# A bias table made by one product of rounded numbers over 97 stacked rows instead of an fp32 product over 33

## The chip, the cores and the metric

The kernel runs on one core of one Trainium2 chip. The metric is device time in microseconds (us): the median of several executions, beside the time of the kernel before on the same chip. One further execution of each kernel is recorded by the hardware profiler, and the rows below come from that one.

## What is computed

One layer of a decoder block on 512 tokens of width 1024, all in fp32: block-sparse attention beside a pooling mixer, then a gated feed-forward part with a short convolution. The change touches only the bias that attention adds to its logits. It depends on head and distance alone:

```
bias_t = rel_bias.T
bias_own = bias_t[:, t5_bucket(dist_own)]
logit_own = jnp.einsum('bhqd,bhkd->bhqk', qc, k_own) * scale + bias_own
logit_own = jnp.where(dist_own >= 0, logit_own, -jnp.inf)
```

`rel_bias` holds 32 buckets for each of 8 heads.

## The kernel before

Matrix products on TensorE (PE) work on numbers that are split in two: a rounded part (type `fp32r`, "hi") and what the rounding left ("lo"). A product is then three passes, hi times hi, hi times lo, lo times hi (`mm3`, lines 127 to 130), and ScalarE (ACT) makes the hi parts while VectorE (DVE) makes the lo parts, ahead of their use. All instructions of PE, DVE and ACT stand in the order in which the program is written; each engine works through its own row of them. POOL (GpSimd) takes small powers and some DMA issues, SP issues most loads.

The program goes through these stages: the adaLN sums and the projections `p` and `q` (to about 61 us), the projection `k` with the pooling arithmetic and the bias table inside it (61 to 86 us), the projection `v` and the first logits, the eight heads interleaved with the gate projections, the branch products, the output projection, and the feed-forward part from about 315 us on.

The bias table is computed for 640 distances and 8 heads. `table` in memory has 33 rows: a one-hot matrix with the entry -1 at each distance's bucket (row 32 marks the distances that are masked), and beside it the 32 bucket values and 1e30. Lines 332 to 337 put three slots of SBUF aside, `hot_0` (512 columns), `hot_1` (128) and `rel` (8), and SP loads them from `table`. `bias_table()` (lines 210 to 215) makes two products, called `fp` in the trace, of `rel` (33x8, fp32) and `hot` (33x512 and 33x128, fp32). Each goes to a bank of PSUM, ACT copies it to the tile `f`, and POOL issues its DMA to the scratch tensor `fd`, from which each head later reads its bias (`trev`, line 434).

Where it stands: `fill(kgen, us)` hands PE a few steps of the projection `k`. Between those calls the program issues the split of the pooling weights (`pwh`, `pwl`, lines 554 and 555), two pooling groups, the normalised queries `n_q` (`head_norm`, line 385), and then `bias_table()` (line 564), so that the two `fp` products stand in the middle of the k projection's third weight unit. The two banks that `fp` writes are those from which the first and the second `n_q` instruction read: in the built program the first `fp` product waits for the first `n_q`, the second for the second.

Of the kernel before, what the change touches and what calls it, by code (L numbers as in the profile page):

```python
# [7 lines left out]
F32 = mybir.dt.float32  # L8
F32R = mybir.dt.float32r
AF = mybir.ActivationFunctionType  # L10
# [8 lines left out]
H = 8  # L19
# [4 lines left out]
NB = 32  # L24
EPS = 1e-6
WINDOWS = (2, 4, 8, 16)
BIG = 1e30
NF = 640
NG = 16
AW = D + 2  # L30
FIRST = 5.2
# [20 lines left out]
def block_kernel(tc, x, cvec, ada, wtok, wch, pool_w, wbr, wout, wup, wdn, pack, table, out):  # L52
    nc = tc.nc
# [3 lines left out]
    with ctx:  # L57
# [11 lines left out]
        def slot(name, dt=F32, w=512):  # L69
            return sp.tile([P, w], dt, tag="s", name=name)  # L70

        def bank(name):
            return psp.tile([P, 512], F32, tag="b", name=name)
# [11 lines left out]
        plan += [(wtok[8 + i], f"v{i}") for i in range(4)]  # L85
        plan += [(wch[i], f"gate{i}") for i in range(NG)]
        for j in range(8):
            if 8 + j >= NG:
                plan.append((wch[8 + j], f"gate{8 + j}"))
# [117 lines left out]

        fd = dpool.tile([H, NF], F32, name="fd")

        def bias_table():  # L210
            for i, (c0, n) in enumerate(((0, 512), (512, NF - 512))):
                fp = bank(f"fp_{i}")
                nc.tensor.matmul(fp[:H, :n], rb_[: NB + 1, :H], hot[i][: NB + 1, :n], start=True, stop=True)
                nc.scalar.activation(fsb[i][:H, :n], fp[:H, :n], AF.Copy)
                nc.gpsimd.dma_start(fd[:, c0 : c0 + n], fsb[i][:H, :n])

# [92 lines left out]
        for k in range(KT):  # L309
            i = k // 2  # L310
            if k % 2 == 0:
                pw, qw = ready.pop(f"p{i}"), ready.pop(f"q{i}")
            c0 = (k % 2) * 512
# [15 lines left out]
            mm3s([(qps[t], hh[k][:, tslice(t)], hl[k][:, tslice(t)], qw[0][:, ws], qw[1][:, ws])  # L329
                  for t in range(TT)], k == 0, k == KT - 1, late=1)  # L330

        hot = [slot("hot_0"), slot("hot_1")]
        rb_ = slot("rel")
        fsb = [slot("f_0"), slot("f_1")]
        nc.sync.dma_start(rb_[: NB + 1, :H], table[:, NF:])
        for i, (c0, n) in enumerate(((0, 512), (512, NF - 512))):
            nc.sync.dma_start(hot[i][: NB + 1, :n], table[:, c0 : c0 + n])

        def tok_proj(i, ps, name):
            for kk in range(4):  # L340
# [9 lines left out]
        def gate_proj(i, store, name):  # L350
            w = unit(name)
            ps = bank(f"{name}_ps")
            for k in range(KT):
                mm3(ps, w[0][:, tslice(k)], w[1][:, tslice(k)], hh[k], hl[k], k == 0, k == KT - 1)
                yield 0.65
            g = slot(name)
            nc.scalar.activation(g, ps, AF.Copy)
            store[i] = g

        def fill(gen, us):  # L360
            while us > 0:
                c = next(gen, None)
                if c is None:
                    return
                us -= c
# [185 lines left out]
        nc.sync.dma_start(pk[:, C_EARLY:], pack[:, C_EARLY:])  # L551
        nc.sync.dma_start(pwr, pool_w)
        fill(kgen, 1)
        nc.scalar.activation(pwh, pwr, AF.Copy)
        nc.vector.tensor_sub(pwl, pwr, pwh.bitcast(F32))
        fill(kgen, 3)
# [5 lines left out]
        pooling(2)  # L562
        fill(kgen, 1)
        bias_table()
        fill(kgen, 1)
        for g in range(2):
# [36 lines left out]
        def gate_stream():  # L603
            for i in range(NG):
                yield from gate_proj(i, gates, f"gate{i}")

        gg = gate_stream()
        fill(gg, FIRST)
        share = (NG * 5.2 - FIRST) / H
        for h in range(H):  # L610
# [345 lines left out]
def _bucket(d):  # L956
    if d < 16:
        return d
    return min(31, 16 + int(math.log(d / 16) / math.log(8.0) * 16))


def _layout(a):
    f = {k: np.asarray(v) for k, v in a.items()}
    one = lambda k: f[k][0]
    c = np.ascontiguousarray
    arr = {}
    arr["x"] = c(f["x"][0])
    arr["cvec"] = c(f["c"])
    unit = np.zeros((6, D, 1), np.float32)
    unit[[1, 4]] = 1.0  # L970
    arr["ada"] = c(np.concatenate(
        [one("ada_w").T, one("ada_b")[:, None], unit.reshape(6 * D, 1)], axis=1)).reshape(48, P, AW)
    w = one("w_in")
    tok = w[:, :2048].reshape(4, 2, P, 4, 512)
    arr["wtok"] = c(tok.transpose(3, 0, 2, 1, 4)).reshape(16, P, 1024)
    ch = lambda m, kt: m.reshape(kt, P, -1, P).transpose(2, 1, 0, 3)
    arr["wch"] = c(ch(w[:, 2048:], KT)).reshape(16, P, 1024)
    arr["pool_w"] = c(one("pool_w").transpose(1, 0, 2)).reshape(P, 512)
    wa, wb = ch(one("w_branch_attn"), 4), ch(one("w_branch_pool"), 4)
    arr["wbr"] = c(np.concatenate([wa, wb], axis=2)).reshape(8, P, 1024)  # L980
    tokm = lambda m: c(m.reshape(m.shape[0] // 256, 2, P, 2, 512).transpose(0, 3, 2, 1, 4)).reshape(-1, P, 1024)
    arr["wout"] = tokm(one("w_out"))
    up = ch(one("w_up"), KT).reshape(2, NP, P, 1024)
    arr["wup"] = c(up.transpose(1, 0, 2, 3)).reshape(2 * NP, P, 1024)
    dn = one("w_down").reshape(NP // 2, 2, P, 2, 512)
    blocks = np.stack([dn[:, 0, :, 0], dn[:, 0, :, 1], dn[:, 1, :, 1], dn[:, 1, :, 0]])
    blocks = np.concatenate([blocks, np.zeros((4, 2 * NU - NP // 2, P, 512), np.float32)], axis=1)
    arr["wdn"] = c(blocks.reshape(4, NU, 2, P, 512).transpose(0, 1, 3, 2, 4)).reshape(4, NU, P, 1024)
    cols = lambda v: v.reshape(-1, P).T
    qk = lambda k: np.concatenate([one(k), one(k)])[:, None]  # L990
    inv = np.zeros((P, 64), np.float32)
    for g, wd in enumerate(WINDOWS):
        inv[:, 16 * g : 16 * g + 16] = 1.0 / np.minimum(np.arange(16) + 1, wd)
    cw = one("conv_w").reshape(3, 2 * NP, P).transpose(2, 1, 0).reshape(P, -1)
    arr["pack"] = c(np.concatenate(
        [cols(one("norm1_g")), cols(one("norm2_g")), qk("q_norm_g"), qk("k_norm_g"),
         cols(one("pool_scale")), inv, np.eye(P, dtype=np.float32), cw, cols(one("conv_b"))], axis=1))
    hot = np.zeros((NB + 1, NF), np.float32)
    for i in range(NF):
        hot[NB if i < 127 else _bucket(i - 127), i] = -1.0  # L1000
    rb = np.concatenate([f["rel_bias"], np.full((1, H), -BIG, np.float32)], axis=0)
    arr["table"] = c(np.concatenate([hot, rb], axis=1))
    return arr


# [20 lines left out]
```

## Time and profile before

| what | value |
|---|---|
| median of 3 runs | 674.45 us (673.62 to 675.25) |
| the profiled execution | 673.66 us, of which the span is 671.7 us |
| PE busy | 659.7 us, 98% of the span |
| DVE busy | 517.0 us, 77% |
| ACT busy | 332.0 us, 49% |
| POOL busy | 93.3 us, 14% |
| granted TensorE clock | 1.000 in the whole span |

The span is the time from the first to the last instruction of the profiled execution; its own time is 1.96 us more. PE rows are matrix products, PEld rows the loads of their stationary operand, which run beside them. In a row of time the first number is the start in us from the span's start, the second the duration; "x4" means that four like instructions are merged. What stands in brackets is the idle time of that engine before the row, and what ended it.

### The profile page before, as it was taken

What the parts mean: (1) busy time and instruction counts of PE and PEld (TensorE: products, weight loads), DVE (VectorE), ACT (ScalarE), POOL (GpSimd) and SP (SyncE); (2) the same over time, 40 slices, a digit from 0 to 9 for tenths busy, and PEclk for the clock granted to TensorE, in tenths of its full rate; (3) what the DMA queues carried; (4) which work ended last, traced back from release to release, by engine and by line L of the source; (5) the groups of instructions that cost most, each with busy time, mean ns of one, the idle gap of its engine ahead of it and who ended that gap; (6) DMA issues with size and microseconds to landing.
All of it is one profiled execution on the core that took longest, in us unless ns stands there. A gap on an engine that the chain in (4) does not pass through costs nothing.

```text
span 671.7 us, 8748 instructions
## 1 busy us (share of the span) xinstructions
PE 659.7 (98%) x3090; PEld 548.5 (82%) x3090; DVE 517.0 (77%) x854; ACT 332.0 (49%) x532; POOL 93.3 (14%) x125
## 2 busy tenths in 40 slices
PE   6999999999999999999999999999999999999997
PEld 3778788888888787888998888888888888888885
DVE  5795876887877688867578878888777878878774
ACT  6555256766564655504653443424343344767431
POOL 3002140000000054703011111120110001001000
PEclk9999999999999999999999999999999999999999
DMA  8785231354543286693367675966845446867651
GB/s 309 290 344 186 94 128 64 111 170 169 173 147 110 94 182 229 226 354 125 107 212 251 226 253 191 305 226 218 298 142 186 163 151 128 292 224 270 244 182 58
DMA packets 41889, 131.48 MB, mean 196 GB/s; under 512 B 5379, under 2 KB 5548, under 8 KB 41846
## 3 DMA queue, kind: packets, MB, share of 16 engines
q1 hardware_dynamic: 35270, 109.82, 48.8%
q0 software_dynamic: 6576, 21.12, 9.4%
q8 instruction: 24, 0.39, 0.2%
q14 instruction: 19, 0.16, 0.1%
HBM read 115.16 MB, written 15.76 MB: 195 GB/s over the span
## 4 chain that ended last, share of the span: by engine, by line
PE 90%; DVE 3%; DMA 3%; ACT 2%; issue 2%; SPq 0%; DVEq 0%; ACTq 0%
PE u L128 12%; PE u L130 12%; PE u L129 12%; PE gate_ps L129 4%; PE gate_ps L128 4%; PE gate_ps L130 4%; PE X L893 3%; PE X L891 3%; PE X L892 3%; PE o L128 2%; PE o L129 2%; PE o L130 2%; DMA raw_ada<-in_ada 2%; DVE raw_ada L191 2%; PE O L495 2%
## 5 line engine op out<-in xcount | busy, mean ns | idle before, releaser
L128 PE MATMUL u<-h2h,hi_up 128*128 128x512 f32 (+1 forms) x384 | 142.7, 372 | 0.0
L129 PE MATMUL u<-h2l,hi_up 128*128 128x512 f32 (+1 forms) x384 | 142.6, 371 | 0.0
L130 PE MATMUL u<-h2h,lo_up 128*128 128x512 f32 (+1 forms) x384 | 142.6, 371 | 0.0
L130 PEld LDWEIGHTS u<-h2h,lo_up 128*128 128x128 f32 x384 | 72.3, 188 | 12.6
L129 PEld LDWEIGHTS u<-h2l,hi_up 128*128 128x128 f32 x384 | 72.3, 188 | 12.5
L128 PEld LDWEIGHTS u<-h2h,hi_up 128*128 128x128 f32 x384 | 72.3, 188 | 12.4
L191 DVE CUSTOM_DVE_ANT_0 raw_ada<-raw_ada,cbc 128x1026 f32<-128x1026 f32 x48 | 58.8, 1250 | 6.1 <-DMA raw_ada<-in_ada 3.2
L761 ACT ACTIVATE uv<-u,pk 128x512 f32<-128x512 f32 x22 | 17.2, 780 | 85.8 <-PE u L130 85.8
L119 DVE TENSOR_TENSOR lo_up<-raw_up,hi_up 128x1024 fp32r<-128x1024 f32 x44 | 52.0, 1218 | 4.8 <-ACT hi_up L109 4.8
L130 PE MATMUL gate_ps<-h_h,lo_gate 128*128 128x512 f32 x128 | 49.9, 390 | 0.0
L129 PE MATMUL gate_ps<-h_l,hi_gate 128*128 128x512 f32 x128 | 49.9, 390 | 0.0
L128 PE MATMUL gate_ps<-h_h,hi_gate 128*128 128x512 f32 x128 | 49.9, 390 | 0.0
L109 ACT ACTIVATE hi_up<-raw_up 128x1024 fp32r<-128x1024 f32 x44 | 44.2, 1048 | 4.3 <-PE u L129 4.3
L814 POOL DMA_DIRECT2D tsum_t<-b x44 | 23.8, 540 | 145.1 <-DVE b L809 139.0
L762 DVE SCALAR_TENSOR_TENSOR uv<-u,pk,uv 128x511 f32<-128x511 f32 x22 | 16.5, 749 | 34.2 <-ACT uv L761 34.2
L119 DVE TENSOR_TENSOR lo_t<-raw_t,hi_t 128x1024 fp32r<-128x1024 f32 (+1 forms) x24 | 26.6, 1131 | 9.1 <-ACT hi_t L109 9.1
L761 ACT ACTIVATE ug<-u,pk 128x512 f32<-128x512 f32 x22 | 17.0, 775 | 32.2 <-PE u L130 32.2
L109 ACT ACTIVATE hi_t<-raw_t 128x1024 fp32r<-128x1024 f32 (+1 forms) x24 | 23.7, 987 | 17.9 <-PE Y L893 8.8
L204 POOL TENSOR_TENSOR wo_l<-raw_wo,wo_h 128x512 fp32r<-128x512 f32 x16 | 25.6, 1621 | 20.2 <-ACT wo_h L203 20.2
L130 PEld LDWEIGHTS gate_ps<-h_h,lo_gate 128*128 128x128 f32 x128 | 24.0, 188 | 5.1
L128 PEld LDWEIGHTS gate_ps<-h_h,hi_gate 128*128 128x128 f32 x128 | 24.0, 188 | 4.6
L129 PEld LDWEIGHTS gate_ps<-h_l,hi_gate 128*128 128x128 f32 x128 | 24.0, 188 | 4.5
(253 smaller groups left out, 1505.4 us busy)
## 6 DMA issues: line engine op xcount, KB each, us to landing
raw_ada<-in_ada SPq DMA_DIRECT2D x48, 513.0 KB, 5.0
raw_up<-in_wup SPq DMA_DIRECT2D x44, 512.0 KB, 4.9
b<-in_wdn SPq DMA_DIRECT2D x44, 256.0 KB, 5.9
tsum_t<-b POOLq DMA_DIRECT2D x44, 256.0 KB, 3.0
raw_t<-tsum_t SPq DMA_DIRECT2D x20, 512.0 KB, 4.5
raw_gate<-in_wch SPq DMA_DIRECT2D x16, 512.0 KB, 5.0
raw_b<-in_wdn SPq DMA_DIRECT2D x15, 512.0 KB, 3.8
raw_br<-in_wbr SPq DMA_DIRECT2D x8, 512.0 KB, 4.4
```

The source lines that it names most:

```text
L109: nc.scalar.activation(hi, raw, AF.Copy)
L119: nc.vector.tensor_sub(lo, raw, hi.bitcast(F32))
L128: nc.tensor.matmul(ps, sh, mh, start=start, stop=False)
L129: nc.tensor.matmul(ps, sh, ml, start=False, stop=False)
L130: nc.tensor.matmul(ps, sl, mh, start=False, stop=stop)
L191: nc.vector.tensor_tensor_reduce(out=raw, in0=raw, in1=cbc, op0=ALU.mult, op1=ALU.add, scale=1.0, scalar=0.0, accum_out=acol[:, i : i + 1])
L204: (eng or nc.vector).tensor_sub(lo[:, :w], src, hi[:, :w].bitcast(F32))
L761: nc.scalar.activation(t, ps, AF.Identity, scale=cw(2), bias=col(C_CB + i))
L814: nc.gpsimd.dma_start(tsum[n, i][:, u * 512 : u * 512 + 512], b[nm])
L891: nc.tensor.matmul(ps, sh, mh, start=start, stop=False, skip_group_check=True)
L892: nc.tensor.matmul(ps, sh, ml, start=False, stop=False, skip_group_check=True)
L893: nc.tensor.matmul(ps, sl, mh, start=False, stop=stop, skip_group_check=True)
```

## The change

The table in memory becomes 97 rows: the 33 rows, 31 rows of zeros, and the 33 rows again. SP loads all 97 of them, the one-hot part to new slots `hotr`. ACT rounds the 97x8 bucket values to `rels`; DVE overwrites rows 64 to 96 of `rels` with what the rounding left. DVE also copies the one-hot parts to `fp32r` (its entries are 0 and -1). The products then take 97 rows in which rounded part and low part meet the same one-hot matrix, so that one product of rounded numbers adds both.

```
+NT = 64 + NB + 1
...
-                nc.tensor.matmul(fp[:H, :n], rb_[: NB + 1, :H], hot[i][: NB + 1, :n], start=True, stop=True)
+                nc.tensor.matmul(fp[:H, :n], rbs[:NT, :H], hot[i][:NT, :n], start=True, stop=True)
...
-        hot = [slot("hot_0"), slot("hot_1")]
+        hot = [slot("hot_0", F32R), slot("hot_1", F32R)]
+        hotr = [slot("hotr_0"), slot("hotr_1")]
+        rbs = slot("rels", F32R)
         rb_ = slot("rel")
         fsb = [slot("f_0"), slot("f_1")]
-        nc.sync.dma_start(rb_[: NB + 1, :H], table[:, NF:])
+        nc.sync.dma_start(rb_[:NT, :H], table[:, NF:])
         for i, (c0, n) in enumerate(((0, 512), (512, NF - 512))):
-            nc.sync.dma_start(hot[i][: NB + 1, :n], table[:, c0 : c0 + n])
+            nc.sync.dma_start(hotr[i][:NT, :n], table[:, c0 : c0 + n])
...
         fill(kgen, 1)
+        nc.scalar.activation(rbs[:NT, :H], rb_[:NT, :H], AF.Copy)
+        nc.vector.tensor_sub(rbs[64:NT, :H], rb_[64:NT, :H], rbs[64:NT, :H].bitcast(F32))
+        for i, n in enumerate((512, NF - 512)):
+            nc.vector.tensor_copy(hot[i][:NT, :n], hotr[i][:NT, :n])
         nc.scalar.activation(pwh, pwr, AF.Copy)
         nc.vector.tensor_sub(pwl, pwr, pwh.bitcast(F32))
...
-    arr["table"] = c(np.concatenate([hot, rb], axis=1))
+    tab = np.concatenate([hot, rb], axis=1)
+    arr["table"] = c(np.concatenate([tab, np.zeros((64 - NB - 1, NF + H), np.float32), tab], axis=0))
```

On DVE the three added instructions stand between the low part of the third k unit (`lo_k`) and that of the pooling weights (`pwl`). Before:

```order
L375 TENSOR_SCALAR hs_q_639<-hs_q_639 128x8
L119 TENSOR_TENSOR lo_k_655<-raw_k_651,hi_k_653 128x1024
L555 TENSOR_TENSOR pwl<-pwr,pwh 128x512
L520 TENSOR_TENSOR pd_1_680<-pt_608 128x511
L521 COPY pd_1_680<-pt_608 128x1
```

and in the changed kernel:

```order
L379 TENSOR_SCALAR hs_q_642<-hs_q_642 128x8
L120 TENSOR_TENSOR lo_k_658<-raw_k_654,hi_k_656 128x1024
L559 TENSOR_TENSOR rels<-rel,rels 33x8
L561 CAST hot_588<-hotr_590 97x512
L561 CAST hot_589<-hotr_591 97x128
L563 TENSOR_TENSOR pwl<-pwr,pwh 128x512
L524 TENSOR_TENSOR pd_1_687<-pt_611 128x511
L525 COPY pd_1_687<-pt_611 128x1
```

All that follows on DVE, `n_q` among it, stands three instructions later; nothing else has moved there. On ACT one instruction (`rels`, 97x8) stands between the rounded parts of that k unit and of the pooling weights.

On PE the two products keep their place in the k projection; in brackets are the semaphores that each waits for (DMAHW: a load). Before:

```order
L130 MATMUL k_646<-hi_k_653,h_l 128x512
L213 MATMUL fp_793<-hot_588,rel 8x512 [waits DMAHW7_49,DMAHW6_49,DVE_49]
L213 MATMUL fp_797<-hot_589,rel 8x128 [waits DMAHW0_49,DVE_49]
L128 MATMUL k_647<-hi_k_653,h_h 128x512
```

and in the changed kernel:

```order
L131 MATMUL k_649<-hi_k_656,h_l 128x512
L214 MATMUL fp_800<-hot_588,rels 8x512 [waits DVE_49,Activation_49]
L214 MATMUL fp_804<-hot_589,rels 8x128 [waits DVE_49]
L129 MATMUL k_650<-hi_k_656,h_h 128x512
```

Neither product waits for a load any more; both wait for DVE as before, the first also for ACT's `rels`. SP's and POOL's queues hold the same instructions in the same order, three of SP's loads with 97 rows in place of 33.

## Rows read from the trace of the kernel before

**Rows 1.** The page: span, PE's busy time, and the chain that ended last by engine.
```profile
span 671.7 us, 8748 instructions
...
PE 659.7 (98%) x3090; PEld 548.5 (82%) x3090; DVE 517.0 (77%) x854; ACT 332.0 (49%) x532; POOL 93.3 (14%) x125
...
PE 90%; DVE 3%; DMA 3%; ACT 2%; issue 2%; SPq 0%; DVEq 0%; ACTq 0%
```

**Rows 2.** Waits of PE in the whole span, longest and shortest: us, times, longest.
```profile
PE cb L230 <- ACT crow L150: 3.2, 1, 3.2
...
PE B L130 <- DVE lo_br L119: 0.2, 1, 0.2
```

**Rows 3.** PE in order of time around the bias products: the first k product, then 77 to 80.6 us.
```profile
61.68 0.39 PE L128 MATMUL k<-hi_k,h_h 128*128 128x512 f32 x1
...
77.10 0.39 PE L130 MATMUL k<-hi_k,h_l 128*128 128x512 f32 x1
77.42 1.24 PE L213 MATMUL fp<-hot,rel 33*8 33x512 f32 x4
78.59 0.50 PE L128 MATMUL k<-hi_k,h_h 128*128 128x512 f32 x1
78.92 0.40 PE L129 MATMUL k<-lo_k,h_h 128*128 128x512 f32 x1
...
80.30 0.39 PE L129 MATMUL pw<-pool_l,pwh 128*128 128x512 f32 x1
```

**Rows 4.** PE in order of time, the narrow products of rounded numbers of one head.
```profile
124.52 0.22 PE L495 MATMUL O<-PT_h,v 128*128 128x128 f32 x1
124.58 0.27 PE L495 MATMUL O<-PT_l,v 128*128 128x128 f32 x1
124.69 0.33 PE L495 MATMUL O<-PT_h,v 128*128 128x256 f32 x1
```

**Rows 5.** Waits from 60 to 100 us: the loads of `fp` for the normalised queries.
```profile
PEld fp L213 <- DVE n_q L385: 0.7, 2, 0.4
```

**Rows 6.** DVE instructions grouped by shape: total us, mean ns, idle before.
```profile
L385 DVE TENSOR_TENSOR n_q<-q,hr_q 128x512 f32<-128x512 f32 x4 | 2.5, 679 | 0.0
L468 DVE TENSOR_SCALAR L<-L,ri 128x128 f32<-128x128 f32 x8 | 2.3, 287 | 0.3
...
L555 DVE TENSOR_TENSOR pwl<-pwr,pwh 128x512 fp32r<-128x512 f32 x1 | 0.7, 689 | 0.0
L107 DVE CAST hi_p<-raw_p 128x1024 fp32r<-128x1024 f32 x1 | 0.7, 687 | 0.0
...
L526 DVE TENSOR_TENSOR fx<-pd,pk 128x2 f32<-128x2 f32 x1 | 0.2, 160 | 0.0
```

**Rows 7.** DVE in order of time, 63 to 98 us.
```profile
63.34 0.17 DVE L375 TENSOR_SCALAR hs_q<-hs_q 128x8 f32<-128x8 f32 x1
...
66.18 0.69 DVE L555 TENSOR_TENSOR pwl<-pwr,pwh 128x512 fp32r<-128x512 f32 x1
...
75.18 2.47 DVE L385 TENSOR_TENSOR n_q<-q,hr_q 128x512 f32<-128x512 f32 x4
...
97.08 0.74 DVE L415 SCALAR_TENSOR_TENSOR Q<-T_True,qgn,Q 64x512 fp32r<-64x512 f32 x1 [2.04 <-ACT Q L414]
```

**Rows 8.** ACT in order of time, 64 to 69 us.
```profile
64.08 0.65 ACT L554 ACTIVATE pwh<-pwr 128x512 fp32r<-128x512 f32 x1
68.57 0.63 ACT L203 ACTIVATE pool_h<-pool 128x512 fp32r<-128x512 f32 x1 [3.84 <-DVE pool L527]
```

**Rows 9.** SP's queue in order of time: the loads of the one-hot matrix.
```profile
51.16 0.72 SPq L337 DMA_DIRECT2D hot<-in_table  x2
```

**Rows 10.** DMA issues: KB each, median us to landing; the pooling weights.
```profile
pwr<-in_pool_w SPq DMA_DIRECT2D x1, 256.0 KB, 6.6
```

**Rows 11.** DVE in order of time, where the branch stage begins.
```profile
228.54 0.69 DVE L204 TENSOR_TENSOR PT_l<-PT,PT_h 128x512 fp32r<-128x512 f32 x1 [2.32 <-ACT PT_h L203]
```

**Rows 12.** POOL in order of time: the powers for the queries.
```profile
62.87 6.88 POOL L377 TENSOR_TENSOR hr_q<-hs_q,mhalf 128x8 f32<-128x8 f32 x4 [48.72 <-DVE hs_q L375]
```

## The prediction

> **What bounds the kernel now.** I read the page first. PE is busy for 659.7 of the 671.7 us and the chain that ended last is PE for 90% [rows 1]: the end moves by what PE's own stream of instructions gains or loses, and hardly by anything else. Then the waits of PE: seven groups in the whole span, the longest 3.2 us at the start, the shortest 0.2 us [rows 2], and none of them at the bias products. So the question is how long the two `fp` products hold PE, and whether what the change puts on DVE makes PE wait where it does not wait now. For the first I read PE in order of time around them, for the second DVE's own stream up to the `n_q` instructions that `fp` stands behind.
>
> **What the products cost now.** In the k projection 69 products of 512 columns start from 61.68 to 77.10, one every 0.227 us, so behind the last of them the next place is 77.33. The eighth product behind `fp` starts at 80.30 [rows 3]; without `fp` it would start at 77.33 + 7 x 0.227 = 78.92. The two fp32 products therefore cost PE 80.30 - 78.92 = 1.38 us. They are four passages in the trace ("x4", 1.24 us).
>
> **What they cost after.** Their operands are then of the type of the k projection, so 512 columns should take the 0.227 us of a k product. For 128 columns the nearest rows are the narrow products of attention: starts 0.06 and 0.11 us apart [rows 4], so rounded numbers do not become slow at 128 columns. What I can't read is what the change of shape costs on either side. Lower bound: 0.227 + 0.06 = 0.29 us. Upper bound: the product behind `fp` now starts 0.33 instead of 0.227 us ahead of its successor [rows 3], and I allow that 0.10 us on both sides and 0.11 for the narrow one: 0.227 + 0.11 + 0.20 = 0.54 us. I take 0.40, the middle. **Term: 1.38 - 0.40 = 0.98 us less on PE**, between 0.84 and 1.09.
>
> The Trainium skill has another way to that term: "FP8 and Floating Point Precision", section "TensorE Precision Notes", says that a true fp32 product takes four passes through the array. With one pass in place of four, 3 x 640 columns at the 0.443 ns a column of a k product go away, an estimate of 0.85 us; the row has 1.38 us where four such passes would be 1.13, so the rule misses what the switch costs, and I stay with the rows.
>
> **What is added on DVE.** Three instructions ahead of `pwl`, at 66.2 us. The subtraction on 33x8: 0.16 us, as the small ones [rows 6]. The copies to `fp32r` are not there in this shape; the nearest is the copy of 1024 columns, 687 ns, and a one-input instruction of 128 columns, 287 ns [rows 6]. The line through these two gives 0.45 ns a column: 0.46 us for 512 and 0.29 for 128, together with the subtraction 0.91 us at most, since DVE starts the next instruction some 0.08 us ahead of the end of the last (four `n_q` of 0.68 us take 2.47, so they start 0.60 apart [rows 6, 7]). I take 0.7 us. Lower bound: the 640 columns alone and the subtraction, 0.29 + 0.16 = 0.45 us; upper bound, if the copies went at the pace of a two-input instruction (689 ns for 512 columns [rows 6]), 0.16 + 0.69 + 0.29 = 1.14 us. DVE has no wait for others here that would swallow this: its pooling arithmetic goes to and fro with ACT, which waits for it for 3.84 us [rows 8]. So all of it arrives at `n_q`.
>
> **What hides it.** The first `n_q` runs from 75.18 to 75.86, the second ends at 76.46 [rows 7]. The first `fp` product can't start before 77.33, the second, 512 columns later, not before 77.56. Slack: 1.47 and 1.10 us. The wait that the trace puts on `n_q` is that of the loads of `fp`'s stationary operand, 0.7 us in two [rows 5]; PE itself does not wait, and 76.46 lies far ahead. With 0.7 us on DVE, `n_q` ends at 77.16: hidden, with 0.4 us to spare. At the upper bound it would be 77.60, 0.04 us late. If the cover were gone, each further us on DVE would be one on PE. Behind `fp`, DVE's lateness ends at 97.08, where it waits 2.04 us for ACT, which waits for PE's transposes [rows 7].
>
> The other additions cost nothing. ACT rounds 97x8 ahead of `pwh` at 64.08, some 0.2 us, and then waits 3.84 us for DVE anyway [rows 8]. The loads carry 97 rows for 33, 165 KB more; they are issued at 51.2 us [rows 9] and wanted at 66.2, and 256 KB issued in this stretch landed in 6.6 us [rows 10].
>
> **Does the gain reach the end?** PE's waits after 80 us are 0.2 us each [rows 2]. The one stage in which DVE and ACT lead, the branch products from 228 to 264 us, starts with DVE idle for 2.32 us, released by ACT behind PE's transposes [rows 11]; it starts earlier by what PE gains.
>
> **The sum.** 673.66 us of the profiled execution - 0.98 = 672.7. The median of the runs is 674.45, 0.8 above that execution; I predict for the median: 674.45 - 0.98 = **673.4 us**, -0.15%. About 0.2%, 1.35 us, is what a measurement of this kernel can tell from no change; its three runs lie 1.6 us apart.
>
> **Rivals.**
>
> *The copies stand behind POOL* (slower). At 66.3 us, when DVE comes to the copies, POOL works on the powers `hr_q`, from 62.87 until 69.75 [rows 12]. If a one-input copy could not run until POOL is done, DVE would be late by 69.75 - 66.3 + 0.7 = 4.1 us, the second `n_q` would end at 80.6 instead of 76.46, and PE, ready at 77.56, would stand for 3.0 us: 674.45 - 0.98 + 3.0 = 676.5 us. It decides from 1.10 us of lateness on, and the kernel is slower from 1.10 + 0.98 = 2.1 us on. Against it: three one-input `hs_q` instructions (the first at 63.34) run in those same 6.88 us and take 0.17 us each [rows 7, 12]; they have 8 columns only. The rule behind it is in the Trainium skill, "SBUF — State Buffer", section "Who interferes with whom": a copy or cast on VectorE may take the port pair that it shares with GpSimd, whoever issues first has it for the whole instruction, and the other is blocked. No row here shows a long copy beside a power. Chance 0.08.
>
> *The gain is lost again in a later stage*: DVE, 77% busy, leads somewhere and doesn't start earlier. For it: the 0.2 us for `lo_br` at the end of the branch stage [rows 2]. Against it: the 2.32 us of rows 11. The time would be 674.4 us. Chance 0.08.
>
> *The change doesn't do what it says*: with 8 output rows and 97 stacked rows the product still goes in four passages and costs 1.38 us. Against it, all other products of rounded numbers, at 0.227 us. 674.4 us. Chance 0.04.
>
> **How the numbers follow.** The forecast holds 0.80. Within it the scatter decides what a measurement calls it: 0.37 us more gain than the forecast would be over 0.2%, so 0.18 of the 0.80 goes to faster, 0.60 to same and 0.02 to slower. The two rivals at 674.4 us give 0.02 to faster, 0.09 to same and 0.01 to slower; POOL's gives 0.07 to slower and 0.01 to same. Faster 0.20, same 0.70, slower 0.10. The range: the forecast with its bounds is 673.3 to 673.6, the scatter of a median adds 0.8 either way, and the two rivals at 674.4 with 0.8 reach 675.2: 672.3 to 675.2. POOL's rival and the tails are left out.
>
> **What the profile would show.** Right: the `fp` row as two passages, and 0.3 to 0.5 us between the last k product before it and the place of the next; copies of some 0.4 and 0.25 us on DVE at 66 us; `n_q` 0.5 to 0.9 us later; no wait of PE at `fp`; everything from 80 us on about 1 us earlier. Wrong: `fp` in four passages, a copy of more than 1 us or an idle DVE beside POOL's powers, a wait of PE for `n_q`, or a branch stage that starts earlier but ends at the old time.

## The result and the profile after

| | before | after |
|---|---|---|
| median of the runs compared | 674.45 us (673.26 to 675.25) | 677.95 us (677.85 to 680.31) |
| profiled execution, span | 673.66, 671.7 us | 677.85, 675.6 us |

Ratio 1.0066, 95% interval 1.0055 to 1.0077: **slower by 0.66%** (the medians lie 3.50 us apart), outside the range, against a forecast of a small gain. The page of the changed kernel: PE is as busy as before within 2 us, but PE's part of the chain that ended last fell from 90% [rows 1] to 79%, and the parts of DMA, DVE and ACT grew.

```profile
span 675.6 us, 8746 instructions
PE 661.6 (98%) x3088; PEld 550.0 (81%) x3088; DVE 517.7 (77%) x857; ACT 331.8 (49%) x533; POOL 92.9 (14%) x125
PE 79%; DMA 8%; DVE 6%; ACT 3%; issue 2%; SPq 1%; POOL 0%; DVEq 0%; ACTq 0%
```

PE in order of time around the bias products, which answers to [rows 3] (start us, duration us, engine, line, instruction; in brackets the idle time ahead of it and its releaser):

```profile
start us, us, engine line op out<-in xcount [idle before <-releaser]
77.28 0.39 PE L131 MATMUL k<-hi_k,h_l 128*128 128x512 f32 x1
80.11 0.79 PE L214 MATMUL fp<-hot,rels 97*8 97x512 f32 x2 [2.44 <-DVE n_q L389]
80.69 0.74 PE L129 MATMUL k<-hi_k,h_h 128*128 128x512 f32 x1
81.22 0.63 PE L130 MATMUL k<-lo_k,h_h 128*128 128x512 f32 x1
...
82.93 0.55 PE L131 MATMUL k<-hi_k,h_l 128*128 128x512 f32 x1
83.31 0.40 PE L129 MATMUL pw<-pool_h,pwh 128*128 128x512 f32 x1
83.55 0.39 PE L130 MATMUL pw<-pool_l,pwh 128*128 128x512 f32 x1
```

Most of the loss can be read here, with the same counting as in the prediction. The next place behind the last k product is 77.28 + 0.23 = 77.51, and without `fp` the eighth product would start at 79.10. It starts at 83.55, so `fp` costs 4.45 us where it cost 1.38: 2.60 us of standing, 0.58 us for the products (two passages now), and 1.27 us in the products behind them, which start 0.43 us apart until 82.93 and not 0.23. The granted clock over the same stretch says why these are so slow:

```profile
core 0: us, PE busy (x) PEld busy (x) DVE busy (x) ACT busy (x) POOL busy (x), PEclk, DMA share, GB/s
78.00:80.00 2.00, 0.00 (x0) 0.00 (x0) 1.87 (x3) 1.05 (x2) 0.00 (x0) 0.96 0.00 0
80.00:83.00 3.00, 2.89 (x8) 1.99 (x9) 3.00 (x5) 0.00 (x0) 0.00 (x0) 0.50 0.51 175
83.00:86.00 3.00, 3.00 (x14) 2.51 (x13) 2.86 (x9) 0.00 (x0) 0.00 (x0) 0.96 0.49 175
```

PE stood, then ran at 0.50, the 1.2 GHz level, and was back near 1.0 behind 83 us. 4.45 - 1.38 = 3.07 us; with 0.18 us by which this run was late already ahead of `fp`, PE is 3.25 us behind at the eighth product and keeps that, within 0.1 us, until 576 us. There it loses 0.7 us more, in the down projection; none of the profiles read below shows a loss there, and its cause stays open. The half clock isn't part of every execution: one of the five has a granted clock of 1.000 and takes 677.95 us, no less than the others.

Why was `n_q` late? ACT and DVE ahead of it, where the split of the pooling weights `pwh`, `pwl` stood at 64.08 and 66.18 [rows 7, 8]:

```profile
start us, us, engine line op out<-in xcount [idle before <-releaser]
66.49 0.16 DVE L559 TENSOR_TENSOR rels<-rel,rels 33x8 fp32r<-33x8 f32 x1
66.67 0.56 DVE L561 CAST hot<-hotr 97x512 fp32r<-97x512 f32 x2
...
69.62 0.63 ACT L562 ACTIVATE pwh<-pwr 128x512 fp32r<-128x512 f32 x1 [5.13 <-DMA pwr<-in_pool_w]
70.28 0.69 DVE L563 TENSOR_TENSOR pwl<-pwr,pwh 128x512 fp32r<-128x512 f32 x1 [3.05 <-ACT pwh L562]
...
79.28 2.48 DVE L389 TENSOR_TENSOR n_q<-q,hr_q 128x512 f32<-128x512 f32 x4
```

The added DVE work took what was forecast (0.7 us), and lies in time that DVE would have stood anyway: behind it DVE waits 3.05 us more, because the load of `pwr` had not landed. SP's queue in order of time (columns as above), which issued the one-hot loads in 0.72 us before [rows 9]. What followed them before:

```profile
51.98 3.42 SPq L77 DMA_DIRECT2D raw_v<-in_wtok  x3
55.45 0.42 SPq L552 DMA_DIRECT2D pwr<-in_pool_w  x1
```

and in the changed kernel:

```profile
51.00 0.28 SPq L339 DMA_DIRECT2D rel<-in_table  x1
51.34 2.87 SPq L341 DMA_DIRECT2D hotr<-in_table  x2
54.30 7.03 SPq L78 DMA_DIRECT2D raw_v<-in_wtok  x3
61.38 0.52 SPq L556 DMA_DIRECT2D pwr<-in_pool_w  x1
```

`pwr` is issued 5.9 us later; the first of the three `raw_v` issues alone takes 5.73 us, where each took 0.33 to 0.35 before. From 55 to 60 us the DMA engines are all but idle. Stretches of the changed kernel (columns as above; the last two are the DMA share and GB/s):

```profile
54.00:56.00 2.00, 2.00 (x11) 1.65 (x10) 1.89 (x3) 0.38 (x1) 0.00 (x0) 1.00 0.15 54
56.00:58.00 2.00, 2.00 (x10) 1.67 (x9) 0.00 (x0) 0.00 (x0) 0.00 (x0) 1.00 0.07 26
58.00:60.00 2.00, 2.00 (x10) 1.67 (x9) 0.00 (x0) 1.33 (x3) 0.00 (x0) 1.00 0.07 26
60.00:62.00 2.00, 2.00 (x10) 1.65 (x10) 0.00 (x0) 1.35 (x4) 0.00 (x0) 1.00 0.61 229
```

and of the kernel before:

```profile
54.00:56.00 2.00, 2.00 (x10) 1.67 (x9) 1.11 (x2) 0.00 (x0) 0.00 (x0) 1.00 0.98 300
56.00:58.00 2.00, 2.00 (x10) 1.67 (x9) 0.00 (x0) 0.00 (x0) 0.00 (x0) 1.00 0.89 281
```

A share of 0.07 is one engine of 16 (0.0625). In the trace's list of DMA packets the 97 rows of the 512-column load, 2 KB each, follow one another, one every 0.08 us, from 54.04 to 61.88 us. **Theory:** the 97 rows all travel on one DMA engine, since 97 is prime; SP stands in the issue of its next loads while that engine takes them in; so `pwr` lands late, the pooling arithmetic and `n_q` behind it are late, and PE stands and falls to half clock. **Rivals:** the added copies delay `n_q`; or the stacked product itself costs the time.

The Trainium skill has the rule, in "DMA: Bandwidth & Descriptors", section "Why a DMA increments its semaphore by 16 and not by 1": the number of engines of a load is the largest one up to 16 that divides the size of its slowest dimension on both sides; 127 partitions get one. By that rule 33 rows use 11 engines and 97 use one; for the 97 the share of 0.07 agrees.

### The profile page after: what moved, and what is told of

Same layout as the page of the kernel before. It is cut to its first block, busy times and chain, and to the rows that moved or that the text cites. A ratio compares the mean times of both kernels' runs of the same rounds, so it can differ in the third digit from the quotient of the medians.

```text
span 675.6 us, 8746 instructions
## 1 busy us (share of the span) xinstructions
PE 661.6 (98%) x3088; PEld 550.0 (81%) x3088; DVE 517.7 (77%) x857; ACT 331.8 (49%) x533; POOL 92.9 (14%) x125
## 4 chain that ended last, share of the span: by engine, by line
PE 79%; DMA 8%; DVE 6%; ACT 3%; issue 2%; SPq 1%; POOL 0%; DVEq 0%; ACTq 0%
PE u L131 11%; PE u L130 11%; PE u L129 11%; PE gate_ps L130 4%; PE gate_ps L129 4%; PE gate_ps L131 4%; PE X L899 2%; PE X L901 2%; PE X L900 2%; PE o L129 2%; PE o L131 2%; PE o L130 2%; DMA raw_b<-in_wdn 2%; DMA raw_ada<-in_ada 2%; DMA raw_br<-in_wbr 2%
```

## The experiments

The times below are medians; before stood at 673.9 to 674.1 us beside them. Except where said, each is the changed kernel with the edit shown.

**Another row count.** The first load line of each edit; the two of the one-hot matrix likewise, and the table gets rows of zeros. The product keeps 97 rows.

```diff
-        nc.sync.dma_start(rb_[:NT, :H], table[:, NF:])
+        nc.sync.dma_start(rb_[:98, :H], table[:, NF:])
```

> The three table loads move 98 rows (one more row of zeros), the product and the copies stay at 97. Theory (97 rows all travel on one DMA engine of 16, SP's next issues stand behind it, the pool_w load, the pooling powers, n_q and so the bias product come late): 98 rows spread over several engines, DMA share from 54 to 60 us back at 0.8 or more, the pool_w issue back near 55.5 us, the first product of the table waits for no n_q; 673.4 us (672.8 to 674.4), so about 1 us below the kernel before. Rival 1 (the added copies on VectorE and ScalarE make n_q late): 677.5 to 678.5, no change from the changed kernel. Rival 2 (the rounded product over 97 rows itself costs the time or the clock): 677 to 678.5 with the issue of pool_w early.

Measured: 673.38 us, ratio to before 0.9993 (0.9985 to 1.0002). Its profiled execution took 1445.93 us, so its views say nothing of the others, and what was expected of the DMA share and of `pwr` is read in the next run. One row of zeros more takes the ratio from 1.0066 to 0.9993, with the same copies and the same product: neither can be the cause.

> As the run with 98 rows, with 112 rows loaded (15 rows of zeros more). Theory: spread over all 16 engines, the same 673.4 us (672.8 to 674.4) as with 98 rows, within 0.3 us of it, since a load that is spread lies under others. If the bytes and not the spread had been the matter, this one would be the slowest of all: 15 percent more bytes than the changed kernel, 678 us or more.

Measured: 673.79 us, 0.9993 (0.9982 to 1.0004). It moves 15% more bytes than the changed kernel and loses nothing. It lies 0.41 us from the run with 98 rows, where 0.3 was expected; the ratios are equal. The DMA share from 54 us on is 0.88, 0.91, 0.91 in its three stretches of 2 us, `pwr` is issued at 56.06. PE around `fp`:

```profile
77.81 0.39 PE L131 MATMUL k<-hi_k,h_l 128*128 128x512 f32 x1
78.03 0.45 PE L214 MATMUL fp<-hot,rels 97*8 97x512 f32 x2
78.32 0.46 PE L129 MATMUL k<-hi_k,h_h 128*128 128x512 f32 x1
...
80.01 0.39 PE L130 MATMUL pw<-pool_l,pwh 128*128 128x512 f32 x1
...
87.78 0.50 PE L129 MATMUL v<-hi_v,h_h 128*128 128x512 f32 x1 [0.34 <-DVE pl_l L541]
```

The next place is 78.04, the eighth product would start at 79.63 and starts at 80.01: `fp` costs **0.38 us**, and the product's gain is 1.00 us. But the last row is a new wait, at the start of the v projection, on `pl_l`, DVE's evacuation of the pooled products. It costs 0.50 us from product to product, and 0.61 with the product behind it, which starts 0.33 us later and not 0.227. DVE's `pl_l`, and the v product that waits for it here, in the kernel before:

```profile
85.48 1.40 DVE L537 SCALAR_TENSOR_TENSOR pl_l<-pw,pk,pl_h 128x512 fp32r<-128x512 f32 x2
87.56 0.39 PE L128 MATMUL v<-hi_v,h_h 128*128 128x512 f32 x1
```

and `pl_l` in this run:

```profile
86.97 1.41 DVE L541 SCALAR_TENSOR_TENSOR pl_l<-pw,pk,pl_h 128x512 fp32r<-128x512 f32 x2
```

**The loads alone.** The kernel before, with its three loads taking 97 rows:

```diff
-        nc.sync.dma_start(rb_[: NB + 1, :H], table[:, NF:])
+        nc.sync.dma_start(rb_[:97, :H], table[:, NF:])
```

> The kernel before, with nothing changed but that its three table loads take 97 rows (the fp32 product still reads 33 of them; no copy, no rounding, no low part). Theory (one engine, SP stands): slower by 2 to 4 us, 676.5 to 678.5, with the pool_w issue after 60 us and PE waiting 1.5 to 2.5 us for n_q ahead of the product. Rivals 1 and 2 (added copies, or the new product): no change, 674.2 to 674.8.

Measured: 678.92 us, 1.0069 (1.0054 to 1.0084), 0.4 us above the expected range: the loads alone make the whole loss: 4.9 us, where the change, with its faster product, lost 3.5. SP's queue and PE in its profile:

```profile
51.18 3.26 SPq L337 DMA_DIRECT2D hot<-in_table  x2
54.54 7.12 SPq L77 DMA_DIRECT2D raw_v<-in_wtok  x3
61.72 0.47 SPq L552 DMA_DIRECT2D pwr<-in_pool_w  x1
...
80.27 1.24 PE L213 MATMUL fp<-hot,rel 33*8 33x512 f32 x4 [1.61 <-DVE n_q L385]
```

`n_q` starts at 79.53, as late as in the changed kernel (79.28). PE waits 1.61 us and not 2.44 because in this execution it came 0.99 us later to the place (its last k product starts at 78.27 for 77.28); the granted clock was 0.50 from 19.0 to 22.4 us here, long before the table's loads were issued. From the first k product to the last v product, 48.75 us before, it takes 2.03 us more.

**The product alone.** 112 rows loaded and copied, but the product again in fp32 over 33 rows of the raw table:

```diff
-                nc.tensor.matmul(fp[:H, :n], rbs[:NT, :H], hot[i][:NT, :n], start=True, stop=True)
+                nc.tensor.matmul(fp[:H, :n], rb_[: NB + 1, :H], hotr[i][: NB + 1, :n], start=True, stop=True)
```

> 112 rows loaded, all added copies kept, but the product is the fp32 one over 33 rows of the raw table, as before (the copies feed nothing). Theory: 674.4 us (674.1 to 675.0), the kernel before plus nothing that can be measured, since the added 0.9 us of VectorE and ScalarE lie in slack; so the run with 112 rows is 0.6 to 1.0 us faster than this one, which is the worth of the product alone. Rival 1: 677 to 678.5.

Measured: 674.03 us, 1.0002 (0.9993 to 1.0011), 0.1 us below the expected range: the additions cost nothing that can be measured as long as PE is not early. The run with 112 rows is only 0.24 us faster by the medians, not 0.6 to 1.0: of the 1.00 us at `fp`, 0.61 go back at `pl_l`, for which PE does not wait in this run. The traces agree: from the first k product to the last v product this run takes 0.00 us more than before, the one with 112 rows 0.41 less.

**Which part of the lateness counts.** First `pool_w` on another queue:

```diff
-        nc.sync.dma_start(pwr, pool_w)
+        nc.scalar.dma_start(pwr, pool_w)
```

> The changed kernel with its 97-row loads as they are, and one thing moved: the load of pool_w is issued by ScalarE's queue and not by SP's, so it no longer stands behind the table and the three raw_v loads. Theory (SP's queue stands behind the one engine): raw_v is still issued late, but pool_w lands before 66 us, the split of it waits for nothing, the product waits for no n_q, 673.8 us (673.0 to 674.6). Rival (the one busy DMA engine holds back every load that needs it, whichever queue issues it, or the added copies matter): pool_w lands after 68 us all the same, 677 to 678.5.

Measured: 676.13 us, 1.0036 (1.0022 to 1.0050): between both theories, since ScalarE itself came to the issue only at 61.22 us, behind two of its `sq_q`. It landed 6.3 us after its issue, as in the run with 112 rows, though the table's 128-column load was still on its way: it was late because it was issued late. `pwh` started at 67.50, 2.1 us before the changed kernel's, and PE waited 1.18 us for `n_q` and 0.63 for `pl_l`:

```profile
78.00 0.74 PE L214 MATMUL fp<-hot,rels 97*8 97x512 f32 x2 [1.18 <-DVE n_q L389]
78.57 0.44 PE L129 MATMUL k<-hi_k,h_h 128*128 128x512 f32 x1
...
80.23 0.39 PE L130 MATMUL pw<-pool_l,pwh 128*128 128x512 f32 x1
```

The granted clock stayed at 1.00. The two products take 0.57 us here too (0.58 in the changed kernel), but those behind them only 0.07 us more than their pace, for 1.27: so 1.20 us of the changed kernel's loss belong to the half clock. This run tells that the time follows `pwr`, but not what of the stall matters. So `pool_w` on SP's queue, ahead of the table:

```diff
+        pwr = slot("pwr")
+        nc.sync.dma_start(pwr, pool_w)
         nc.sync.dma_start(rb_[:NT, :H], table[:, NF:])
...
-        pwr = slot("pwr")
...
-        nc.sync.dma_start(pwr, pool_w)
```

> The changed kernel with its 97-row loads as they are, and the load of pool_w issued on SP's queue ahead of the table's loads instead of behind raw_v; no other engine's order changes. It repeats the question that the run with pool_w on ScalarE's queue left open, since ScalarE issued it only at 61.2 us, no earlier than SP in the changed kernel. Theory (of all that stands behind the one engine, only pool_w's lateness reaches TensorE): pool_w is issued near 51 us and landed before 60, the raw_v loads are as late as in the changed kernel, no wait of the product for n_q, a wait of 0.3 us for pl_l as in the run with 112 rows, 673.8 us (673.2 to 674.6). Rival (the late raw_v loads or the busy engine matter too): 675 us or more, with a new wait of the v projection or of n_q.

Measured: 673.89 us, 1.0000 (0.9991 to 1.0009). As expected, PE does not wait for `n_q`, and waits 0.34 us for `pl_l`. SP's queue and the stretches show that the stall itself is still there:

```profile
50.58 0.42 SPq L340 DMA_DIRECT2D pwr<-in_pool_w  x1
...
54.72 11.47 SPq L78 DMA_DIRECT2D raw_v<-in_wtok  x4
```

```profile
56.00:58.00 2.00, 2.00 (x10) 1.65 (x9) 0.00 (x0) 0.00 (x0) 0.00 (x0) 1.00 0.07 28
58.00:60.00 2.00, 2.00 (x11) 1.65 (x10) 0.00 (x0) 1.96 (x4) 0.00 (x0) 1.00 0.07 26
```

So the raw weights of v may be late; of all that stood behind the one engine only `pool_w` reached PE.

**The table by GpSimd's queue:** all three loads with `nc.gpsimd` for `nc.sync`.

> The changed kernel with its 97-row loads as they are, issued by GpSimd's queue and not by SP's, earlier in the program. Theory: raw_v and pool_w are issued by SP as in the kernel before (pool_w at about 55.5 us), no wait of the product for n_q, 673.8 us (673.0 to 674.6), though the table still goes by one engine. Rival (any load that goes by one engine delays the transfers of the others that use it): DMA share low after 54 us, 676 us or more.

Measured: 674.70 us, 1.0010 (1.0001 to 1.0019), 0.1 us above the range. SP issues `pwr` at 55.84 as before and no product waits for `n_q`, as the theory had it. But one thing that the expectation took for granted is not so:

```profile
12.01 0.61 POOL L339 DMA_DIRECT2D rel<-in_table  x1
12.62 1.09 POOL L341 DMA_DIRECT2D hotr<-in_table  x2
```

POOL came to these issues at 12 us, and by the list of DMA packets the 512-column table moved from 16.0 to 17.9 us, in packets of 4 and 2 KB, up to nine at a time: neither by one engine nor beside `raw_v` and `pool_w`. So the run shows that the loss goes when the table leaves SP's queue; its rival it does not try. From the first k product to the last v product it gains 0.39 us, the run with 112 rows 0.41; where the 0.9 us between their medians come from is not settled.

**A middle dose:** 106 rows, 2 times 53.

> The changed kernel with 106 rows loaded, 2 times 53 with 53 prime, so by the theory two engines with 53 rows each. Theory (what counts is how long SP's queue stands): twice the DMA share of the changed kernel in the stall (0.13 for 0.07), half its length, pool_w issued near 57 us and landed near 65 us, just in time for ScalarE, so no wait of the product for n_q: 673.8 us (673.0 to 674.6). Rival (any row count that does not fall on nearly all engines loses the same, or the row count above 96 does): 677 us or more.

Measured: 674.70 us, 1.0005 (0.9995 to 1.0015); a little above the range, and the expectation of no wait was wrong. Issue of `pwr`, start of `pwh`, PE's wait at `fp`, and the time from the first k product to the last v product less the 48.75 us of before, each from that run's profile, all with the stacked product:

| run | `pwr` issued | `pwh` starts | PE waits for `n_q` | first k to last v | median |
|---|---|---|---|---|---|
| 97 rows, `pool_w` first | 50.58 | 63.73 | 0 | -0.34 | 673.89 |
| 112 rows | 56.06 | 64.88 | 0 | -0.41 | 673.79 |
| 106 rows | 57.65 | 67.38 | 0.48 | +0.76 | 674.70 |
| 97 rows, `pool_w` by ScalarE | 61.22 | 67.50 | 1.18 | +1.57 | 676.13 |
| 97 rows (the change) | 61.38 | 69.62 | 2.44 | +3.06 | 677.95 |

The later `pwh`, the more is lost, but it counts against where PE is by then: the third and the fourth run start it 0.12 us apart, and PE came to `fp` 0.58 us earlier in the fourth (its last k product starts at 76.42 for 77.00). I had the two engines right (the packets of the 512-column load run two at a time for most of 55.0 to 58.5 us) and the issue time with them (57 expected, 57.65 measured), not the landing: 9.7 us after the issue, where 256 KB landed in 6.3 with 112 rows, so it landed at 67.4 and not near 65.

**The DVE work earlier.** 112 rows, and the four added instructions ahead of the head sums of q, where DVE stood for `sq_q` (6.72 us in the kernel before):

```diff
+        nc.scalar.activation(rbs[:NT, :H], rb_[:NT, :H], AF.Copy)
+        nc.vector.tensor_sub(rbs[64:NT, :H], rb_[64:NT, :H], rbs[64:NT, :H].bitcast(F32))
+        for i, n in enumerate((512, NF - 512)):
+            nc.vector.tensor_copy(hot[i][:NT, :n], hotr[i][:NT, :n])
         qr = head_sums(qps, "q")
...
```

> 112 rows loaded, and the rounding, the low part and the two copies written ahead of the head sums of q, where VectorE waited 6.7 us for sq_q, instead of behind them. Theory (in the run with 112 rows the product gained 0.9 us, and 0.3 to 0.5 us of it went to a wait of the v projection for pl_l, which VectorE ends later by the added 0.7 us): no wait for pl_l, 673.3 us (672.7 to 673.8), about 0.5 us below the run with 112 rows. Rival (that wait has another cause): 673.8 us and the wait is still there.

Measured: **672.61 us, 0.9981 (0.9973 to 0.9990)**: the only run whose whole interval lies below 1, and better than both kernels. It is 0.1 us below the range that was expected, and 1.2 us below the run with 112 rows where 0.5 was expected. DVE in its profile:

```profile
60.73 0.56 DVE L554 CAST hot<-hotr 97x512 fp32r<-97x512 f32 x2
61.70 0.69 DVE L378 TENSOR_REDUCE hs_q<-sq_q 128x8 f32<-128x512 f32 x1 [0.40 <-ACT sq_q L376]
...
75.05 2.48 DVE L389 TENSOR_TENSOR n_q<-q,hr_q 128x512 f32<-128x512 f32 x4
```

`n_q` starts at 75.05, with no lateness left (75.18 before [rows 7]), `fp` again costs 0.38 us, and the wait for `pl_l` is gone. From the first k product to the last v product it gains 1.05 us, 0.64 more than the run with 112 rows. This run alone has the gain that the prediction put to the change; that its median gains 1.5 us (0.7 to 1.8 by the interval) and not 1.05 is not explained by its trace.

## Why the prediction was wrong

- **The step that failed:** "The loads carry 97 rows for 33, 165 KB more; they are issued at 51.2 us [rows 9] and wanted at 66.2, and 256 KB issued in this stretch landed in 6.6 us [rows 10]", costed at nothing. I compared bytes with the landing time of a load of 128 rows and took for granted that 97 rows travel as that does. I also asked only whether the table comes in time, which it did; I did not ask what stands behind it on SP's queue. Three loads of `raw_v` and `pool_w` did, and `pool_w` was issued 5.9 us later. The run with the 97-row loads alone (678.92) against the full change with 98 rows (673.38), and the run with `pool_w` ahead of the table (673.89), show it.
- **A rival was missing.** The Trainium skill's rule on the number of engines, cited above, speaks against this change and has no place in the prediction.
- **The price of a late `n_q` was half there.** The prediction said that behind the cover each us on DVE is one on PE, and its slower rival had the second `n_q` end at 80.6 and PE stand for 3.0 us. In the changed kernel it ends at 80.56 (79.28 + 0.60 + 0.68), by another cause, and PE stands 2.60 us. What the forecast left out is the 1.20 us that the half clock then costs in this execution, and that the two products cost 0.64 us behind a stand even at full clock (0.57 and the 0.07 behind them, in the run with `pool_w` by ScalarE), where they cost 0.38 without one.
- **The rival's cause fell.** The copies were not blocked beside POOL's powers: they took 0.56 us together from 66.67, while POOL's `hr_q` ran from 63.06 to 69.55. The rule of the Trainium skill quoted there has no effect that these rows show.
- **The product's term was right:** 0.40 us forecast for `fp`, 0.38 measured where PE does not wait (112 rows, the DVE work earlier, `pool_w` first); 0.98 us of gain, 1.00 measured. That the bounds held is no luck; that the middle of them hit within 0.02 us is. The product goes in two passages, so that rival fell too.
- **The DVE term was right in size, and its cover only at `fp`.** 0.7 us forecast; `n_q` starts 0.78 us later against PE's last k product with 112 rows, and no wait at `fp`. But "behind `fp`, DVE's lateness ends at 97.08" passed over `pl_l` at 87 us. Before, the first `pl_l` ended 1.38 us ahead of the v product that waits for it with 112 rows (85.48 + 0.70 = 86.18, the product at 87.56). With 112 rows `pl_l` starts at 86.97, 1.49 us later, and PE comes there 0.28 us earlier: 1.77 us, 0.39 more than there was. So the rival "the gain is lost again in a later stage" was partly right, at a place that I had not read.
- **Does the gain reach the end?** Not all of it, in these traces. At the end of the branch stage PE waits for `lo_br` 0.5 us in most of these runs and 0.2 before [rows 2]. From the first to the last product on the bank `B` that stage takes 41.11 us before, 41.2 in the changed kernel and with `pool_w` first, and 41.5 to 41.9 in the others, also in the run that only has longer loads and in the one that keeps the fp32 product. So it does not go with the size of the gain. The latter run's median equals that of before all the same, so the one traced execution of the kernel before may not be typical there. The cause stays open.

## What to carry to other kernels

Cost a load by its row count before its bytes: look for the share of the DMA engines while it runs, and if it is one sixteenth, add a row of zeros so that the count divides well. Then read what stands behind that load on its queue, since a load that is itself in time can make another one late. When a change speeds up one engine and burdens another, look for the next place where the two meet, not only the first: there the gain and the added work add up.

## What the runs showed that I had not expected

- One load of 97 rows, 194 KB, moves at 26 GB/s (shares of 0.07) while others of 256 to 512 KB stand behind it on the queue; SP needs 7.03 us to issue three loads that took 3.42 us before.
- PE fell to a granted clock of 0.50 behind a stand of 2.44 us, and lost 1.20 us by it. Behind stands of 1.18 us, and of 1.61 us ahead of the fp32 product, it did not: the k products behind these are 0.23 us apart and the granted clock is 1.00. The length of a stand does not tell it alone: with 112 rows loaded the clock was 0.50 from 18.2 to 21.6 us, where the last stand before, ahead of 16.2 us, had been 0.9 us; in the run with 112 rows and the fp32 product a stand of 2.0 us in that place left it at 1.00.
- A copy of 97x512 to rounded numbers takes 0.43 us and one of 97x128 takes 0.22 on DVE beside a working POOL; the line through other shapes had given 0.46 and 0.29.
